# The first layer's gate in block form: half of its contraction as seven block products in place of eight

## Chip, core and metric

One core of one Trainium2 chip runs the whole program. The metric is the device time of one execution in microseconds (us). The engines are TensorE (PE in the profile), VectorE (DVE), ScalarE (ACT), GpSimd (POOL) and SyncE (SP); the last two issue most DMAs.

## What is computed

Two decoder layers over 512 tokens of width 1024 in float32. Layer 0 mixes tokens with a Mamba-2 SSD, layer 1 with HGRN2. Behind each mixer come a squared-ReLU MLP and a gated embedding:

```python
h = layer_norm(ALPHA * x + mix, ln_g[i, 0], ln_b[i, 0])
h = layer_norm(ALPHA * h + sq_relu_mlp(h, w1[i], w2[i]), ln_g[i, 1], ln_b[i, 1])
x = h + sigmoid(h @ ple_w_gate[i]) * (p[i] @ ple_w_proj[i])
```

The change is in the last line for i = 0: the gate's product h @ ple_w_gate is 512x1024 by 1024x1024, and the projection of p has a contraction of 256.

## The kernel before

**Products.** Every float32 matrix is split in two float32r parts, hi (a rounded copy, made by ScalarE) and lo (the difference, made by VectorE). A product is three matmuls, hi by hi, hi by lo and lo by hi (mm3, L120 to L122), 128 contraction rows by 128 tokens by 512 columns each. A weight unit is 128x1024: SyncE loads it into one of three buffers raw, then split makes whi (L113, ScalarE) and wlo (L116, VectorE) in rings of six. PSUM has four banks pj and one each of pt, pm, py0 and py1.

**Block products.** The MLP's second product, the value projection (values4) and the last layer's gate (last_gate) use seven products of matrix blocks in place of eight (Strassen's scheme as Winograd orders it). It needs sums of weight blocks and sums of token blocks. weight_sums loads weight blocks with GpSimd's DMAs (L329) into the eight buffers r and sums them on VectorE (L336, L339, L340, L344). last_gate makes its four sums t3, t1, t2, t4 in the DMAs themselves: GpSimd issues them with an adding or copying DMA each (L401 to L408), and a link that adds to a buffer waits for the DMA that filled it.

**The gate of layer 0 before.** The end of mlp_and_gate runs two halves of 512 columns by four chunks of 128 tokens; each has 24 matmuls of the gate and 6 of the projection. Behind the next chunk's matmuls the finished chunk of x is transposed (turn, L625), four transposes for half a row, and split into x_n, with a plain copy in rows for values4's block sums. **The gate of layer 1**, last_gate, takes half of the contraction in seven block products (part), the other half directly (rest), and holds partial results in cells. The pair sums of h come from kept, a copy that transpose_split makes (L245).

**Around it.** The last period of the MLP's second product gives the layer norm its chunks: product accumulates into acc with row sums (L373), layer_norm finishes chunk by chunk (L213 to L224), and turned yields the transposes of h (L238, split on ScalarE in L242 and on VectorE in L243) between the gate's first matmuls. values4, the first part of layer 1, runs right behind layer 0's gate and needs its own weight sums.

**Order.** The engines run their queues in order. A list scheduler sets each engine's order ahead of the run by priorities (high_priority with LEAD 100, SOON 40 and so on) and its own estimates of durations; the part of the order that the change touches is shown below. A tile's buffer is given out when its last user is done.

Of the kernel before, what the change touches and what calls it, by code (L numbers as in the profile page):

```python
# [15 lines left out]
P = 128  # L16
T = 512
# [27 lines left out]
def trunk(ctx: ExitStack, tc, a):  # L45
# [351 lines left out]
    def last_gate(wp, wg, h_s, p_s, kept, turned):  # L397
# [13 lines left out]
        cells = [mk(b8, [P, 4, T], "b8") for _ in range(3)] + [tmp("blk", [P, 4, T])]  # L411
        cell = lambda n: cells[n // 4][:, n % 4, :]
# [36 lines left out]
        def final(c, h, g, pp, pin=None):  # L449
# [3 lines left out]
            for ps, cs in pp:  # L453
# [5 lines left out]
                nc.sync.dma_start(a["out"][tok(c), fs], acc[:, c, fs])  # L459
# [46 lines left out]
        raw = mk(raws, [P, 1024], "raw")  # L506
        pu = mk(w4, [P, 1024], "a", F32R), mk(w4, [P, 1024], "b", F32R)
        with tc.high_priority(offset=LEAD):
            nc.sync.dma_start(raw, wp[1])
            nc.scalar.copy(pu[0], raw)  # L510
            nc.vector.tensor_sub(pu[1], raw, f32(pu[0]))
# [15 lines left out]
        for u in range(2):  # L527
# [3 lines left out]
            final(2 + u, 0, cell(6 + u), [(cell(2 + u), whole)])  # L531
        for u in range(2):
# [25 lines left out]
    def mlp_and_gate(layer, h_s, last):  # L558
# [36 lines left out]
        for g, period in enumerate(PERIODS):  # L595
            if g < 4:
                tiles = hidden(g)
            if g > 0:
                if g == 4:
                    kept = tmp("blk", [P, 2, 4, 256]) if last else None  # L600
# [12 lines left out]
        if last:  # L613
            return last_gate(a[f"wp_{layer}"], a[f"wg_{layer}"], h_s, p_s, kept, turned)

        x_n = Split(8)
        rows = [tmp("blk", [P, 2, 4, 256]) for _ in range(2)]
        late = []

        def turn(h, c):  # L620

            sl = slice(c * P, (c + 1) * P)
            pt = bank(pst, "pt")
            for j in range(4):
                nc.tensor.transpose(pt[:, j * P : (j + 1) * P], acc[:, c, h * 512 + j * P : h * 512 + (j + 1) * P], ident)  # L625
            v = pt.rearrange("p (j t) -> p j t", j=4)
            hh = x_n.hi[h][:, :, sl]
            nc.scalar.copy(hh, v)
            nc.scalar.copy(rows[c // 2][:, h, :, c % 2 * P : (c % 2 + 1) * P], v)
            nc.vector.tensor_sub(x_n.lo[h][:, :, sl], v, f32(hh))  # L630

        pps = {}

        def proj(c, pu):

            ps = pps[c] = bank(*((psj, "pj") if c > 1 and pps else (psy, "py%d" % (c % 2))))
            sl = slice(c * P, (c + 1) * P)
            for k in range(2):
                ks = slice(k * 512, (k + 1) * 512)
                mm3(ps, p_s[0][:, k, sl], p_s[1][:, k, sl], pu[0][:, ks], pu[1][:, ks], k == 0, k == 1)  # L640

        for h in range(2):
            pu = unit(a[f"wp_{layer}"][h])
            gu = [unit(a[f"wg_{layer}"][4 * h + j]) for j in range(4)]
            for c in range(NCH):
                sl = slice(c * P, (c + 1) * P)
                if h == c == 0:
                    turns = turned(1)
                    for i in range(NCH):
                        proj(i, pu)  # L650
                        if i in (1, 2):
                            next(turns)
                if h == 1:
                    proj(c, pu)
                turns = turned(c + 2) if h == 0 and c < 2 else None
                pg = bank(psj, "pj")
                sg = tmp("sg", [P, T])
                for k in range(8):
                    ks = slice((k % 2) * 512, (k % 2 + 1) * 512)
                    mm3(pg, h_s.h(k, sl), h_s.l(k, sl), gu[k // 2][0][:, ks], gu[k // 2][1][:, ks], k == 0, k == 7)  # L660
                    if turns and k in (2, 5):
                        next(turns)
                nc.scalar.activation(sg, pg, AF.Sigmoid)
                nc.vector.tensor_mul(sg, pps.pop(c), sg)
                d = acc[:, c, h * 512 : (h + 1) * 512]
                nc.vector.tensor_add(d, sg, d)
                while late:
                    late.pop(0)()
                late.append(lambda h=h, c=c: turn(h, c))
        return x_n, rows, late  # L670

    def values4(xs, rows, late):
# [38 lines left out]
        for f in late:  # L711
            f()
# [751 lines left out]
```

## Time and profile before

| what | value |
|---|---|
| time, median of 3 runs | 1411.65 us (1411.61 to 1413.34) |
| the profiled execution | 1411.34 us |
| its span, first to last instruction | 1409.6 us |
| TensorE busy | 1404.3 us, 8001 matmul records |
| VectorE busy | 1069.1 us |
| ScalarE busy | 763.6 us |
| GpSimd busy | 45.8 us |
| HBM over the span | 127 GB/s |

Times within a profile are counted from the span's start. A line number names the source line of an instruction, and "out<-in" the tiles it writes and reads. The time in square brackets behind a row is how long its engine stood idle before it, and what ended that. Layer 0's gate begins near 696 us and values4 near 760; the last gate is the end of the program, from 1347 us on.

### The profile page before, as it was taken

Reading aid. Unit: us, or ns where it says so; the run is one execution under the profiler, and the core shown is the slowest. Engines: PE = TensorE matmul, PEld = TensorE weight load, DVE = VectorE, ACT = ScalarE, POOL = GpSimd, SP = SyncE. Lnnn points to the kernel's source line nnn. Section 1 sums busy time; section 2 is a strip of 40 time slices with the busy share of each in tenths; the row PEclk is TensorE's granted clock in tenths of the full one; section 3 lists DMA queues with packets and bytes.
Section 4 is the critical chain, followed back from the end, with each engine's and each line's share of the span. In section 5 each row is a group of like instructions: output and inputs, shape, how many; then the busy total and the mean of one; then the engine's idle time right before and its main releaser. Section 6 shows DMA issues by size and latency. Waiting matters only on the chain.

```text
span 1409.6 us, 20400 instructions
## 1 busy us (share of the span) xinstructions
PE 1404.3 (100%) x8001; PEld 1168.1 (83%) x8001; DVE 1069.1 (76%) x1778; ACT 763.6 (54%) x1156; POOL 45.8 (3%) x92
## 2 busy tenths in 40 slices
PE   9999999999999999999999999999999999999998
PEld 7888888888988888888888888888898888888887
DVE  7989688698977668677986577678785867667795
ACT  7766465573354444545555547655555454544573
POOL 0000000001000000000000000000100000000100
PEclk9999999999999999999999999999999999999999
DMA  8433333234433444345621421222443444444731
GB/s 313 135 117 120 106 120 110 85 100 156 141 113 127 157 131 152 129 142 178 209 90 49 134 91 61 76 87 96 150 135 105 147 137 148 144 137 159 202 106 60
DMA packets 50399, 181.69 MB, mean 129 GB/s; under 512 B 5632, under 2 KB 6400, under 8 KB 50176
## 3 DMA queue, kind: packets, MB, share of 16 engines
q1 hardware_dynamic: 38784, 138.45, 29.6%
q0 software_dynamic: 11520, 41.95, 9.2%
q8 instruction: 63, 1.03, 0.3%
q14 instruction: 32, 0.26, 0.1%
HBM read 177.16 MB, written 2.16 MB: 127 GB/s over the span
## 4 chain that ended last, share of the span: by engine, by line
PE 99%; DMA 0%; DVE 0%; issue 0%; DVEq 0%
PE pj L120 25%; PE pj L121 25%; PE pj L122 25%; PE py L120 5%; PE py L122 5%; PE py L121 5%; PE py L906 1%; PE pt L238 1%; PE py L1175 1%; PE pm L923 1%; PE pm L871 1%; PE py L1301 1%; PE pt L859 0%; PE py L1303 0%; PE py L1240 0%; PE py L832 0%
## 5 line engine op out<-in xcount | busy, mean ns | idle before, releaser
L113 ACT CAST whi<-raw 128x1024 fp32r<-128x1024 f32 x218 | 228.8, 1050 | 333.2 <-PE pj L121 243.6
L120 PE MATMUL pj<-b,whi 128*128 128x512 f32 (+1 forms) x990 | 378.6, 383 | 0.0
L122 PE MATMUL pj<-b,wlo 128*128 128x512 f32 (+1 forms) x990 | 376.8, 381 | 0.0
L121 PE MATMUL pj<-b,whi 128*128 128x512 f32 (+1 forms) x990 | 376.6, 381 | 0.0
L116 DVE TENSOR_TENSOR wlo<-raw,whi 128x1024 fp32r<-128x1024 f32 x218 | 265.4, 1221 | 129.4 <-ACT whi L113 128.2
L121 PEld LDWEIGHTS pj<-b,whi 128*128 128x128 f32 x990 | 186.4, 188 | 34.6 <-issue 0.9
L122 PEld LDWEIGHTS pj<-b,wlo 128*128 128x128 f32 x990 | 186.3, 188 | 34.5
L120 PEld LDWEIGHTS pj<-b,whi 128*128 128x128 f32 x990 | 186.1, 188 | 34.0
L122 PE MATMUL pj<-whi,b 128*128 128x512 f32 x520 | 204.1, 392 | 0.0
L120 PE MATMUL pj<-whi,b 128*128 128x512 f32 x508 | 202.1, 398 | 0.0
L121 PE MATMUL pj<-wlo,b 128*128 128x512 f32 x508 | 199.2, 392 | 0.0
L113 ACT CAST whi<-r 128x1024 fp32r<-128x1024 f32 x76 | 80.0, 1053 | 68.5 <-PE pj L122 39.4
L122 PEld LDWEIGHTS pj<-whi,b 128*128 128x128 f32 x520 | 97.7, 188 | 20.1
L120 PEld LDWEIGHTS pj<-whi,b 128*128 128x128 f32 x508 | 95.5, 188 | 19.1 <-ACT b L1322 0.3
L121 PEld LDWEIGHTS pj<-wlo,b 128*128 128x128 f32 x508 | 95.5, 188 | 18.7 <-issue 0.2
L116 DVE TENSOR_TENSOR wlo<-r,whi 128x1024 fp32r<-128x1024 f32 x76 | 92.5, 1220 | 19.6 <-ACT whi L113 19.1
L122 PE MATMUL py<-whi,b 128*128 128x512 f32 x260 | 101.3, 390 | 0.0
L121 PE MATMUL py<-wlo,b 128*128 128x512 f32 x248 | 96.6, 389 | 0.0
L120 PE MATMUL py<-whi,b 128*128 128x512 f32 x248 | 96.4, 390 | 0.0
L329 POOL DMA_DIRECT2D r<-in_w x64 | 34.0, 532 | 1098.8 <-DVE wlo L116 544.3
L122 PEld LDWEIGHTS py<-whi,b 128*128 128x128 f32 x260 | 48.8, 188 | 10.2
L800 DVE SCALAR_TENSOR_TENSOR cv<-pj,cst,cv 128x509 f32<-128x509 f32 (+2 forms) x66 | 48.9, 746 | 10.6 <-ACT cv L797 9.8
(368 smaller groups left out, 1943.5 us busy)
## 6 DMA issues: line engine op xcount, KB each, us to landing
raw<-in_w SPq DMA_DIRECT2D x112, 512.0 KB, 3.3
r<-in_w POOLq DMA_DIRECT2D x64, 512.0 KB, 3.8
raw<-in_wssd SPq DMA_DIRECT2D x36, 512.0 KB, 3.9
a<-csd SPq DMA_DIRECT2D x16, 512.0 KB, 4.1
raw<-in_wso SPq DMA_DIRECT2D x16, 512.0 KB, 3.3
raw<-in_whq SPq DMA_DIRECT2D x16, 512.0 KB, 3.4
raw<-in_wg SPq DMA_DIRECT2D x15, 512.0 KB, 4.0
raw<-in_whvg SPq DMA_DIRECT2D x14, 512.0 KB, 3.4
```

The costliest lines, as they stand in the source:

```text
L113: nc.scalar.copy(hi[:, :n], f)
L116: nc.vector.tensor_sub(lo[:, :n], f, f32(hi[:, :n]))
L120: nc.tensor.matmul(out, sh, mh, start=start, stop=False, **kw)
L121: nc.tensor.matmul(out, sh, ml, start=False, stop=False, **kw)
L122: return nc.tensor.matmul(out, sl, mh, start=False, stop=stop, **kw)
L238: nc.tensor.transpose(pt[:, j * P : (j + 1) * P], src[:, k * P : (k + 1) * P], ident)
L329: queue.dma_start(t[i][u], src)
L800: nc.vector.scalar_tensor_tensor(cv[:, d:], ps[:, : T - d], convw[:, i, k : k + 1], cv[:, d:], ALU.mult, ALU.add)
L871: nc.tensor.matmul(pst_[:, c * P : (c + 1) * P], btok[:, c, :], xw[:, c].rearrange("p h q -> p (h q)"), start=True, stop=True)
L906: mm = nc.tensor.matmul(yds[0][64 * r : 64 * r + 64, sl], xdt[:, 2 * c + r, :], m[:, r, sl], start=True, stop=True)
L923: mm = nc.tensor.matmul(yo[:, c * P : (c + 1) * P], pv[:, c - 1].rearrange("p h q -> p (h q)"), cm[:, c * P : (c + 1) * P], start=True, st ...
L1175: nc.tensor.matmul(pcs[r][bs, at : at + n], kk[r][:, ts], qs, start=True, stop=True)
```

## The change

last_gate becomes block_gate with an argument last and serves both layers. For layer 0 it keeps the new x in acc in place of writing it out, holds its partial results in two tiles of cells in place of four, computes the projection's second half just before each use, and transposes the new x (turn) between its own products. The two last turns are left to values4, which places them inside its first products. kept exists in both layers now. The layer norm of layer 0 ahead of the gate has priority SOON for all chunks.

```diff
-            with tc.high_priority(offset=LEAD if c == 3 and i % 2 == 0 else 0 if c > 1 and i == 1 else SOON):
+            with tc.high_priority(offset=LEAD if c == 3 and i % 2 == 0 else SOON):
...
-    def last_gate(wp, wg, h_s, p_s, kept, turned):
+    def block_gate(wp, wg, h_s, p_s, kept, turned, last):
...
+        if last:
+            cells = [mk(b8, [P, 4, T], "b8") for _ in range(3)] + [tmp("blk", [P, 4, T])]
+            cell = lambda n: cells[n // 4][:, n % 4, :]
+        else:
+            cells = [mk(b8, [P, 4, T], "b8"), tmp("blk", [P, 4, T])]
+            homes = [(0, 0), (0, 1), (0, 2), (0, 3), (1, 0), (1, 1), (0, 0), (0, 1), (1, 2), (1, 3)]
+            cell = lambda n: cells[homes[n][0]][:, homes[n][1], :]
...
-        raw = mk(raws, [P, 1024], "raw")
-        pu = mk(w4, [P, 1024], "a", F32R), mk(w4, [P, 1024], "b", F32R)
...
-        for n, c in enumerate((2, 3, 0)):
-            ps = bank(psj, "pj")
-            proj(ps, c, pu)
-            nc.scalar.copy(cell(10 + n), ps)
+        if last:
...
         for u in range(2):
+            if not last and u:
+                turn(0, 2)
             part(x[u], summed(2), t1, u, False)
             nc.vector.tensor_add(cell(8 + u), x[u], cell(8 + u))
         us = [negated(wg[6]), negated(wg[7])]
         b22 = unit(wg[5])
+        if not last:
+            pu = unit(wp[1])
+            for u in range(2):
+                g = bank(psj, "pj")
+                rest(g, 2 + u, us, True)
+                nc.vector.tensor_add(cell(8 + u), g, cell(8 + u))
+                ps = bank(psj, "pj")
+                proj(ps, 2 + u, pu)
+                final(2 + u, 1, cell(8 + u), [(ps, whole)])
+                if u == 0:
+                    turn(0, 3)
+            for u in range(2):
+                part(x[u], summed(3), b22, u, False, False)
+                if u:
+                    turn(0, 1)
+                rest(x[u], u, us, False)
+                if u == 0:
+                    turn(0, 0)
+                ps = bank(psj, "pj")
+                proj(ps, u, pu)
+                final(u, 1, x[u], [(ps, whole)])
+                turn(1, 2 + u)
+            return x_n, rows, [lambda: turn(1, 0), lambda: turn(1, 1)]
...
-        x_n = Split(8)
-        rows = [tmp("blk", [P, 2, 4, 256]) for _ in range(2)]
...
-        for h in range(2):
-            pu = unit(a[f"wp_{layer}"][h])
-            gu = [unit(a[f"wg_{layer}"][4 * h + j]) for j in range(4)]
-            for c in range(NCH):
...
+        return block_gate(a[f"wp_{layer}"], a[f"wg_{layer}"], h_s, p_s, kept, turned, last)
...
             for c in range(2):
+                if late and c:
+                    late.pop(0)()
...
-        for f in late:
-            f()
+        late.pop(0)()
```

The source lines shift by the change: L336 to L344, L373 and the L401 to L408 of the sums keep their numbers; the negation of a weight unit (negated) is L425 and L427 before and L430 and L432 after, and the pair sums of h are L497 to L503 before and L503 to L509 after. In the rows below the numbers behind a name tell buffers apart, and a trailing "xn" counts equal rows.

First, GpSimd's queue between the last sums of the MLP and the memory fills of layer 1. r is a buffer of a weight block, in_wg the gate's weight, in_whvg that of the value projection. Before:

```order
L329 DMA r_5542<-in_w_0 128x1024
L329 DMA r_6347<-in_whvg 128x1024
L329 DMA r_6341<-in_whvg 128x1024
L329 DMA r_6343<-in_whvg 128x1024
L329 DMA r_6348<-in_whvg 128x1024
L329 DMA r_6342<-in_whvg 128x1024
L329 DMA r_6344<-in_whvg 128x1024
L329 DMA r_6345<-in_whvg 128x1024
L329 DMA r_6346<-in_whvg 128x1024
```

Now, up to the fourth load of the value projection:

```order
L401 DMA r_5889<-in_wg 128x1024
L403 DMA r_5889<-in_wg 128x1024
L402 DMA r_5890<-in_wg 128x1024
L405 DMA r_5891<-r_5889 128x1024
L404 DMA r_5890<-in_wg 128x1024
L406 DMA r_5891<-in_wg 128x1024
L407 DMA r_5892<-r_5891 128x1024
L329 DMA r_6388<-in_whvg 128x1024
L329 DMA r_6382<-in_whvg 128x1024
L408 DMA r_5892<-in_wg 128x1024
L329 DMA r_6384<-in_whvg 128x1024
L329 DMA r_6389<-in_whvg 128x1024
```

The eight loads of the value projection stood alone there; now the gate's chain stands ahead of them, with two of the loads before its last link and the third behind it.

Second, VectorE's queue at the end of the MLP's second product, at the first sums for the value projection. wlo is the low part of a weight unit, lnsum the row sums of the layer norm, lnmv its mean and variance, pj and py are banks. Before:

```order
L336 TENSOR_TENSOR r_6341<-r_6341,r_6347 128x1024
L336 TENSOR_TENSOR r_6342<-r_6342,r_6348 128x1024
L116 TENSOR_TENSOR wlo_5811<-raw_5807,whi_5809 128x1024
L116 TENSOR_TENSOR wlo_5817<-raw_5813,whi_5815 128x1024
L373 ISA acc_99,lnsum_5530<-pj_5610,acc_99 128x512
L373 ISA lnsum_5530 128x1
L373 ISA acc_99,lnsum_5530<-py_940_5573,acc_99 128x512
L373 ISA lnsum_5530 128x1
L339 TENSOR_TENSOR r_6347<-r_6347,r_6343 128x1024
L116 TENSOR_TENSOR wlo_5897<-raw_5893,whi_5895 128x1024
L213 TENSOR_SCALAR lnmv_5739<-lnsum_5530 128x1
L116 TENSOR_TENSOR wlo_5903<-raw_5899,whi_5901 128x1024
```

Now:

```order
L336 TENSOR_TENSOR r_6382<-r_6382,r_6388 128x1024
L339 TENSOR_TENSOR r_6388<-r_6388,r_6384 128x1024
L116 TENSOR_TENSOR wlo_5812<-raw_5808,whi_5810 128x1024
L116 TENSOR_TENSOR wlo_5818<-raw_5814,whi_5816 128x1024
L373 ISA acc_99,lnsum_5531<-pj_5611,acc_99 128x512
L373 ISA lnsum_5531 128x1
L373 ISA acc_99,lnsum_5531<-py_941_5574,acc_99 128x512
L373 ISA lnsum_5531 128x1
L340 TENSOR_TENSOR r_6384<-r_6382,r_6384 128x1024
L116 TENSOR_TENSOR wlo_5909<-raw_5905,whi_5907 128x1024
L116 TENSOR_TENSOR wlo_5915<-raw_5911,whi_5913 128x1024
L373 ISA acc_99,lnsum_5531<-py_942_5575,acc_99 128x512
```

The second sum there now is L339, which reads the third load (r_6384), where an L336 on the fourth and fifth loads' buffers stood; L340 follows, and the norm's first row (L213) has moved behind the accumulations.

Third, TensorE's queue in layer 0's gate, behind the last transposes of h. whi and wlo are the parts of a weight unit, b the parts of h or of its pair sums, pt a bank of transposes. Before, the end of the second chunk's product with the turn of the first chunk of x:

```order
L122 MATMUL pj_6059<-whi_5919,b_921_5529 128x512
L120 MATMUL pj_6059<-whi_5919,b_919_5527 128x512
L121 MATMUL pj_6059<-wlo_5921,b_919_5527 128x512
L122 MATMUL pj_6059<-whi_5919,b_921_5529 128x512
L625 MATMUL pt_6088<-cst_165,acc_99 128x128 x4
L120 MATMUL pj_6096<-whi_5901,b_918_5526 128x512
L121 MATMUL pj_6096<-wlo_5903,b_918_5526 128x512
L122 MATMUL pj_6096<-whi_5901,b_920_5528 128x512
```

Now, the end of the block product with t2, the first two matmuls of rest with the negated unit, and the block product with t4:

```order
L122 MATMUL py_1031_5983<-whi_6092,b_1005_5901 128x512
L120 MATMUL py_1031_5983<-whi_6092,b_1005_5901 128x512
L121 MATMUL py_1031_5983<-wlo_6094,b_1005_5901 128x512
L122 MATMUL py_1031_5983<-whi_6092,b_1005_5901 128x512
L120 MATMUL pj_6229<-whi_6207,b_920_5528 128x512
L121 MATMUL pj_6229<-wlo_6209,b_920_5528 128x512
L120 MATMUL pj_6104<-whi_6096,b_919_5527 128x512
L121 MATMUL pj_6104<-wlo_6098,b_919_5527 128x512
L122 MATMUL pj_6104<-whi_6096,b_921_5529 128x512
```

Two matmuls of the third chunk's rest, which need the low part wlo_6209 of a negated unit, stand ahead of the block product with t4.

The low part that the second of them reads stands here in VectorE's queue now, behind the sums of pairs (blk) and their low parts (b_1005, b_1006), with no counterpart before:

```order
L504 TENSOR_TENSOR blk_5522<-blk_5522 128x512
L116 TENSOR_TENSOR wlo_6102<-r_5890,whi_6100 128x1024
L499 TENSOR_TENSOR b_1005_5901<-blk_5522,b_1005_5901 128x512
L506 SCALAR_TENSOR_TENSOR blk_5522<-blk_5522 128x512
L499 TENSOR_TENSOR b_1006_5902<-blk_5522,b_1006_5902 128x512
L509 SCALAR_TENSOR_TENSOR blk_5522<-blk_5522 128x512
L499 TENSOR_TENSOR b_1005_5901<-blk_5522,b_1005_5901 128x512
L492 TENSOR_TENSOR blk_5904<-pj_6038,blk_5904 128x512
L336 TENSOR_TENSOR r_6383<-r_6383,r_6389 128x1024
L499 TENSOR_TENSOR b_1006_5902<-blk_5522,b_1006_5902 128x512
L461 TENSOR_TENSOR sg_6084<-b_1007_5903,sg_6084 128x512
L432 SCALAR_TENSOR_TENSOR wlo_6209<-raw_6205,whi_6207 128x1024
```

L432 is the twelfth row from L504, with a sum for the value projection (L336) and the first gate result (L461) ahead of it.

More of the change, by code (lines that the diff above doesn't have):

```diff
@@ L504, in last_gate @@
             put(3, a12)
[L506 to L515 removed]
+        if last:
+            raw = mk(raws, [P, 1024], "raw")
+            pu = mk(w4, [P, 1024], "a", F32R), mk(w4, [P, 1024], "b", F32R)
+            with tc.high_priority(offset=LEAD):
+                nc.sync.dma_start(raw, wp[1])
+                nc.scalar.copy(pu[0], raw)
+                nc.vector.tensor_sub(pu[1], raw, f32(pu[0]))
+            for n, c in enumerate((2, 3, 0)):
+                ps = bank(psj, "pj")
+                proj(ps, c, pu)
+                nc.scalar.copy(cell(10 + n), ps)
         for u in range(2):
@@ L531, in last_gate, with turn @@
             final(2 + u, 0, cell(6 + u), [(cell(2 + u), whole)])
+        x_n = Split(0)
+        rows = [None, None]
+        def turn(h, c):
+            if len(x_n.hi) == h:
+                x_n.hi.append(mk(b8, [P, 4, T], "b8", F32R))
+                x_n.lo.append(mk(b8, [P, 4, T], "b8", F32R))
+            if rows[c // 2] is None:
+                rows[c // 2] = tmp("blk", [P, 2, 4, 256])
+            pt = bank(pst, "pt") if c % 2 else bank(psm, "pm")
+            for j in range(4):
+                nc.tensor.transpose(pt[:, j * P : (j + 1) * P], acc[:, c, h * 512 + j * P : h * 512 + (j + 1) * P], ident)
+            v = pt.rearrange("p (j t) -> p j t", j=4)
+            hh = x_n.hi[h][:, :, tok(c)]
+            nc.scalar.copy(hh, v)
+            nc.scalar.copy(rows[c // 2][:, h, :, c % 2 * P : (c % 2 + 1) * P], v)
+            nc.vector.tensor_sub(x_n.lo[h][:, :, tok(c)], v, f32(hh))
         for u in range(2):
+            if not last and u:
+                turn(0, 2)
             part(x[u], summed(2), t1, u, False)
@@ L599, in mlp_and_gate @@
                 if g == 4:
-                    kept = tmp("blk", [P, 2, 4, 256]) if last else None
+                    kept = tmp("blk", [P, 2, 4, 256])
                     h_s, after, turned, sums = norm(2 * layer + 1, kept)
```

50 lines of the change are left out of this document (2 added, 48 removed).

## The prediction

> **What bounds the kernel now.** I read the page first: the span, the busy times, the chain that ended last.
>
> ```profile
> span 1409.6 us, 20400 instructions
> ...
> PE 1404.3 (100%) x8001; PEld 1168.1 (83%) x8001; DVE 1069.1 (76%) x1778; ACT 763.6 (54%) x1156; POOL 45.8 (3%) x92
> ...
> PE 99%; DMA 0%; DVE 0%; issue 0%; DVEq 0%
> ```
>
> TensorE (PE) is the whole chain: 99% of it, with no share for a wait. A busy PE need not be a fast one, so next comes PE's timeline at two places, the products of the last gate and the turns before the first one.
>
> ```profile
> 1370.14 0.39 PE L120 MATMUL pj<-a,a 128*128 128x512 f32 x1
> ...
> 1374.22 0.39 PE L120 MATMUL pj<-whi,b 128*128 128x512 f32 x1
> ...
> 695.64 0.39 PE L122 MATMUL py<-whi,blk 128*128 128x512 f32 x1
> 695.87 0.60 PE L238 MATMUL pt<-cst,acc 128*128 128x128 f32 x4
> 696.23 0.48 PE L120 MATMUL py<-whi,blk 128*128 128x512 f32 x1
> 696.54 0.40 PE L121 MATMUL py<-wlo,blk 128*128 128x512 f32 x1
> ```
>
> The first column is the start. Eighteen matmuls lie between 1370.14 and 1374.22: 0.227 us each, start to start. A turn of four transposes with the matmul behind it takes 695.87 to 696.54, so the turn alone costs 0.44 us. These are steps without a wait. What the change saves on PE it saves in full, and whatever makes PE wait is added in full.
>
> Which engine could make it wait is told by the busy time by stretch, around the start of the first gate and the same place in the last one.
>
> ```profile
> 680.00:690.00 10.00, 10.00 (x46) 8.28 (x45) 9.80 (x14) 5.20 (x7) 0.00 (x0) 1.00 0.63 210
> 690.00:700.00 10.00, 10.00 (x48) 8.27 (x47) 10.00 (x19) 6.83 (x13) 0.00 (x0) 1.00 0.63 205
> ...
> 1330.00:1340.00 10.00, 10.00 (x46) 8.28 (x45) 6.53 (x14) 4.57 (x8) 0.86 (x1) 1.00 0.95 312
> ```
>
> After the length come PE, weight loads, VectorE (DVE), ScalarE, GpSimd, PE's clock, DMA share and GB/s. DVE is full ahead of the first gate and has 3.5 us in 10 free ahead of the last, because the sums of the value projection's weights (L336 to L344) run only in the first layer. The last gate's form comes to a place where DVE has nothing to spare.
>
> **Part by part: PE.** The removed gate has 8 chunks (2 halves by 4) of 30 matmuls, 240. The block form has 7 block products of 12, the direct half of the contraction (96) and the projection of p (48): 228. Twelve fewer at 0.227 us are 2.72 us. The turns stay 8 in number. DVE and ScalarE get four more weight splits, the cell copies and the pair sums; these cost nothing where the engine has room, and DVE has none up to the first pair.
>
> **The load that DVE waits for.** The GpSimd queue issues these loads one after another.
>
> ```profile
> 653.38 0.53 POOL L329 DMA_DIRECT2D r<-in_whvg  x1 [19.87 <-DVE wlo L116]
> ...
> 675.03 0.53 POOL L329 DMA_DIRECT2D r<-in_whvg  x1 [1.20 <-DVE wlo L116]
> ...
> 1304.75 0.53 POOL L401 DMA_DIRECT2D r<-in_wg  x1 [20.86 <-DVE wlo L116]
> 1308.75 0.90 POOL L403 DMA_DIRECT2D r<-in_wg  x1 [3.47 <-DMA r<-in_wg]
> ...
> 1320.74 0.87 POOL L406 DMA_DIRECT2D r<-in_wg  x1 [3.87 <-DMA r<-r]
> 1327.10 0.57 POOL L407 DMA_DIRECT2D r<-r  x1 [5.49 <-issue]
> 1333.24 0.86 POOL L408 DMA_DIRECT2D r<-in_wg  x1 [5.57 <-DMA r<-r]
> ```
>
> Today the eight value loads (L329) start from 653.38, as buffers come free; the last is issued at 675.03. The last gate's sums are a chain, each link waiting for the landing before it, from L401 at 1304.75 to L408 at 1333.24. Both start when the same buffers of the last product come free, so the layers lie 1304.75 - 653.38 = 651.37 apart. In the first layer the chain therefore issues L407 at 675.7 and L408 at 681.9, done at 682.7. By the order, two value loads stand ahead of L408 and the third, r_6384, right behind it: it can't be issued before 682.7.
>
> What it takes to land is bounded by these rows: the page's median of such loads, then the answers for L402 and L404 (a plain load issued just behind an accumulating one, and an accumulating one behind a copy).
>
> ```profile
> r<-in_w POOLq DMA_DIRECT2D x64, 512.0 KB, 3.8
> ...
> DMA to landing us min/median/max: 6.2/6.2/6.2
> ...
> DMA to landing us min/median/max: 8.0/8.0/8.0
> ```
>
> r_6384 is a plain load behind the accumulating L408, so I take L402's 6.2 us: it lands at 688.9. The ends are 686.5 and 690.7.
>
> DVE's timeline of before at that place:
>
> ```profile
> 680.46 2.36 DVE L336 TENSOR_TENSOR r<-r,r 128x1024 f32<-128x1024 f32 x2
> 682.73 2.36 DVE L116 TENSOR_TENSOR wlo<-raw,whi 128x1024 fp32r<-128x1024 f32 x2
> ...
> 688.78 0.20 DVE L213 TENSOR_SCALAR lnmv<-lnsum 128x1 f32<-128x1 f32 x1
> ...
> 690.75 0.15 DVE L218 TENSOR_TENSOR lnmv<-lnsq 128x1 f32<-128x1 f32 x1
> 690.82 1.27 DVE L223 SCALAR_TENSOR_TENSOR acc<-acc,lnmv,a 128x1024 f32<-128x1024 f32 x1
> ...
> 692.80 1.28 DVE L224 SCALAR_TENSOR_TENSOR acc<-acc,lnrs,b 128x1024 f32<-128x1024 f32 x1
> ...
> 1368.96 0.68 DVE L243 TENSOR_TENSOR b<-pm,b 128x512 fp32r<-128x512 f32 x1
> 1369.56 0.68 DVE L493 TENSOR_TENSOR b<-blk,b 128x512 fp32r<-128x512 f32 x1
> ```
>
> Steps, start to start: 1.14 us for 1024 columns (680.46 to 682.73 for two), 0.60 for 512 (1368.96 to 1369.56), 1.2 for a layer norm's 1024-wide step. In the new order the second row after 680.46 is an L339 that reads r_6384. Undisturbed it ends at 682.7; with the load at 688.9 it ends at 690.1, 7.4 us later. Behind it wait the splits of the last MLP product's units, the accumulations of its banks and the first chunk's layer norm. From 680.46 undisturbed: seven steps of 1.14 and three of 0.6 to L213, 690.3; 2.0 to the variance (688.78 to 690.75), then three norm steps of 1.2, one of 0.6 and small ones: the norm ends at 696.7. PE reaches the first turn, now six matmuls later than 695.87, at 697.2. So 0.5 us of the 7.4 is covered and **6.9 us** reach PE; with the ends of the landing, 4.5 and 8.7.
>
> **DVE at the first pair.** PE's rows from the first turn to the first block product on a pair are 78 matmuls and 8 turns, 17.7 + 3.5 = 21.2 us. DVE's rows from that norm's end to the last sum before that pair (L504) are 5 of 1.2, 6 of 1.14, 13 of 0.6 and 0.6 us of small ones: 21.3, and the cast on ScalarE behind it takes another 0.6. PE waits 0.9. The last gate doesn't show this wait because its 18 projection matmuls (1370.14 to 1374.22, 4.1 us) stand just there; in the new code they come later. Then PE runs 24 matmuls (5.4 us) and a first one of the negated rest; the second needs L432's output, behind two steps of 1.14 and eight of 0.6 since L504 and itself 1.14: with one 0.7 us wait for a cast, 8.9 us after L504, where PE arrives after 0.8 + 5.7 = 6.5. PE waits 2.4 more. Together **3.3 us**. Ends: 1.0, if one wait of ScalarE shifts and the second disappears, and 4.5, if the following three weight sums also get in the way of the first turn of x.
>
> **The sum.** -2.7 + 6.9 + 3.3 = +7.5 us. The profiled execution took 1411.34 us (1.74 outside the span); its median of three is 1411.65, 0.3 more. Forecast: **1418.8 us**. Its own range: 1411.34 - 2.7 + 4.5 + 1.0 = 1414.1 to 1411.34 - 2.7 + 8.7 + 4.5 = 1421.8.
>
> **The clock.** The 6.9 us fall into pieces. The longest comes after the bank of the first turn's MLP product is free: PE runs six matmuls (1.4 us) while DVE does the norm's 6.4 from L213 to the end, so it stands for 5.0. How PE begins after standing still is seen at the kernel's start.
>
> ```profile
> 0.78 3.36 PE L153 MATMUL pm<-const-float32-0.0 128*128 128x256 f32 x8 [0.78 <-PEq L1452]
> ...
> L153 PE MATMUL pm<-const-float32-0.0 x8: 381/634/767, 0.8 to 3.8; 128*128 128x256 f32 x8
> ```
>
> Eight equal matmuls; most last 634 ns, the last one 381. If PE began so again after the wait, 3.36 us of work at 634 in place of 381 would lose 3.36 x (1 - 381/634) = 1.3 us. The Trainium skill ("TensorE: Matmul & The Clock Gate", Part 1) says that an idle window of about 3.4 us halves PE's clock until it has been busy about as long; by that rule the loss here would be 1.7 us as an estimate from the page. No idle stretch of that length lies inside this trace, so it is a rival and not in the sum.
>
> **Rivals.**
> 1. Faster or even: the waits don't happen, and only the twelve matmuls count, 1408.6. It decides if r_6384 lands by 681.6, when L339 would begin undisturbed. For: the eight value loads are all issued by 675.03 now, and no L336 or L339 of that place waits. Against: six links of the chain would have to be over 7 us shorter in sum than the rows of the last gate, with the same buffers and the same neighbours. 0.12, of which I put 0.07 on just over 0.2% and 0.05 on just under.
> 2. The load comes in time but DVE is late at the first pair: -2.7 + 3.3 = +0.6, 1411.9. For: DVE's full stretch. Against: as under 1. 0.08.
> 3. The forecast and the clock: 1418.8 + 1.3 = 1420.1. For: L153's rows. Against: the wait is split by the rest of an MLP product, and its one long piece is hardly longer than the warm-up of the start. 0.12.
> 4. That PE's matmuls don't get fewer is ruled out by the order, which has twelve fewer of 128x512.
>
> **How the numbers follow.** The forecast has 0.68. Runs of this kernel tell 0.2%, 2.8 us, from no change. Slower: the forecast and rival 3, 0.80. Within 0.2%: rival 2 and part of rival 1, 0.13. Faster: 0.07. The range leaves out rival 1 (0.12) and the tails: from 1411.8, just below rival 2, to 1423.0, the forecast's upper end with the clock's 1.3.
>
> **What would show it.** Right: in the profile after, an L339 of DVE shortly after 680 idle for 5 to 9 us, ended by a DMA of in_whvg; PE idle ahead of the first L238 of the first layer for about as long; L408 of the first layer starting near 682 and the L329 behind it landing near 689; PE waiting 1 us at the first block product with t3 and 2 to 3 us at the first rest with negated weights; 12 matmuls fewer. Wrong: the L339 without idle time before it (the load term falls), the wait there but PE running on (DVE had slack that I didn't see), or PE's steps in this gate longer than 0.227 us without a wait.

## Result and profile after

| what | before | after |
|---|---|---|
| time, median of 5 runs each | 1412.28 us (1411.61 to 1413.34) | 1424.75 us (1424.66 to 1426.14) |
| ratio after to before | | 1.0091, 95% interval 1.0076 to 1.0106 |
| the profiled execution | 1411.34 us | 1426.14 us |

The kernel became 12.5 us slower, 0.9%. The prediction said slower, but by 7 us: 1418.8, with a range up to 1423.0. Three lines of the page after answer to those of before: the span, the busy times, and the chain that ended last.

```profile
span 1423.9 us, 20423 instructions
...
PE 1409.8 (99%) x7989; PEld 1170.0 (82%) x7989; DVE 1081.6 (76%) x1797; ACT 774.4 (54%) x1177; POOL 51.5 (4%) x100
...
PE 48%; DVE 2%; DMA 1%; issue 1%; ACT 0%; POOL 0%; DVEq 0%; POOLq 0%
```

Twelve matmul records fewer (7989, 8001 before), and yet more busy time on PE: some matmuls became longer. The chain, all PE before, now passes through DVE and a DMA. (It could be followed back from the end only to 670.65 us, so its shares add up to about half.) Where it does so, PE's timeline shows (start, duration; in brackets the idle time before and what ended it):

```profile
693.95 0.39 PE L122 MATMUL pj<-whi,b 128*128 128x512 f32 x1
697.57 0.77 PE L120 MATMUL py<-whi,blk 128*128 128x512 f32 x1 [3.23 <-DVE lnsum L373]
698.14 0.63 PE L121 MATMUL py<-wlo,blk 128*128 128x512 f32 x1
...
703.23 0.39 PE L121 MATMUL py<-wlo,blk 128*128 128x512 f32 x1
...
704.15 0.40 PE L122 MATMUL py<-whi,blk 128*128 128x512 f32 x1
707.76 1.11 PE L238 MATMUL pt<-cst,acc 128*128 128x128 f32 x4 [3.21 <-DVE acc L224]
708.53 0.78 PE L120 MATMUL py<-whi,blk 128*128 128x512 f32 x1
...
713.63 0.40 PE L120 MATMUL pj<-whi,a 128*128 128x512 f32 x1
```

Two waits of 3.2 us, and behind each a stretch of slow matmuls: 13 from 697.57 to 703.23 and 12 from 708.53 to 713.63, 0.43 us a step in place of 0.227. The clock column of the stretches agrees (length, PE, weight loads, DVE, ScalarE, GpSimd, clock, DMA share, GB/s):

```profile
680.00:690.00 10.00, 10.00 (x46) 8.29 (x45) 2.81 (x5) 2.11 (x2) 1.96 (x3) 1.00 1.01 339
690.00:700.00 10.00, 6.77 (x26) 5.25 (x25) 7.29 (x10) 2.10 (x2) 0.00 (x0) 0.82 0.57 192
700.00:715.00 15.00, 11.79 (x39) 9.18 (x38) 13.61 (x27) 9.67 (x20) 0.00 (x0) 0.67 0.37 113
```

The first of these rows holds the origin. DVE, full there before, works 2.8 us in 10, and the DMA engines, at 0.63 before, are at 1.01. DVE's timeline says what it waits for, GpSimd's when those loads were issued:

```profile
681.50 0.08 DVE L373 DVE_READ_ACCUMULATOR2_ANT lnsum<- 128x1 f32 x1
687.35 1.23 DVE L336 TENSOR_TENSOR r<-r,r 128x1024 f32<-128x1024 f32 x1 [5.77 <-DMA r<-in_whvg]
692.71 1.23 DVE L339 TENSOR_TENSOR r<-r,r 128x1024 f32<-128x1024 f32 x1 [4.14 <-DMA r<-in_whvg]
...
676.66 0.55 POOL L407 DMA_DIRECT2D r<-r  x1 [5.14 <-DVE wlo L116]
677.29 1.08 POOL L329 DMA_DIRECT2D r<-in_whvg  x2
682.57 0.89 POOL L408 DMA_DIRECT2D r<-in_wg  x1 [4.20 <-DMA r<-r]
683.12 1.41 POOL L329 DMA_DIRECT2D r<-in_whvg  x2
```

Not one sum waits but two. The times from issue to landing of the two pairs of L329:

```profile
DMA to landing us min/median/max: 6.2/7.8/9.5
...
DMA to landing us min/median/max: 9.5/9.9/10.2
```

Three smaller waits follow: at the first block product with t3, at the second matmul of the rest with a negated unit, and at a turn of the new x.

```profile
732.67 0.50 PE L120 MATMUL pj<-whi,b 128*128 128x512 f32 x1 [0.64 <-ACT b L498]
...
740.19 0.50 PE L121 MATMUL pj<-wlo,b 128*128 128x512 f32 x1 [1.31 <-DVE wlo L432]
...
777.16 0.63 PE L551 MATMUL pt<-cst,acc 128*128 128x128 f32 x4 [0.83 <-DVE b L556]
```

**The account.** Steps from start to start, less the 0.227 us of a matmul without a wait: 3.4 and 3.4 for the two waits, 2.7 for the first slow stretch (5.66 for 13 matmuls, less 2.95), 2.7 for the second (0.3 at the transposes, then 5.10 for 12 matmuls, less 2.72), and 0.8, 1.6 and 1.0 at the three small ones: 15.6 us. Less 2.7 for the twelve matmuls that is 12.9, against 12.5 between the medians. The account is that of the profiled execution, whose span is 14.3 us longer than before. Of these, 1.0 lies at the program's start, far from the change: the first L120 begins at 8.57 us there and at 7.59 before. Between two marks, the first py<-whi,blk well ahead of the gate and the first py<-qd,cv behind it, it takes 349.9 us for 336.6 before, 13.3 more; the account explains all but 0.4 of that.

### The profile page after: what moved, and what is told of

Same layout as the page of the kernel before. It is cut to its first block, busy times and chain, and to the rows that moved or that the text cites. A ratio compares the mean times of both kernels' runs of the same rounds, so it can differ in the third digit from the quotient of the medians.

```text
span 1423.9 us, 20423 instructions
## 1 busy us (share of the span) xinstructions
PE 1409.8 (99%) x7989; PEld 1170.0 (82%) x7989; DVE 1081.6 (76%) x1797; ACT 774.4 (54%) x1177; POOL 51.5 (4%) x100
## 4 chain that ended last, share of the span: by engine, by line
PE 48%; DVE 2%; DMA 1%; issue 1%; ACT 0%; POOL 0%; DVEq 0%; POOLq 0%
PE pj L120 12%; PE pj L121 12%; PE pj L122 12%; PE py L122 3%; PE py L121 3%; PE py L120 3%; PE py L1170 1%; DMA r<-in_whvg 1%; PE pt L238 1%; DVE wlo L116 1%; PE py L1296 1%; DMA r<-r 0%; PE py L1298 0%; PE py L1235 0%; PE py L1278 0%
## 5 line engine op out<-in xcount | busy, mean ns | idle before, releaser
L120 PE MATMUL pj<-b,whi 128*128 128x512 f32 (+1 forms) x990 | 378.6, 383 | 0.0
L116 DVE TENSOR_TENSOR wlo<-raw,whi 128x1024 fp32r<-128x1024 f32 x215 | 261.6, 1221 | 130.2 <-ACT whi L113 129.3
L120 PEld LDWEIGHTS pj<-b,whi 128*128 128x128 f32 x990 | 186.2, 188 | 34.3
L122 PE MATMUL pj<-whi,b 128*128 128x512 f32 x504 | 198.0, 393 | 0.0
L120 PE MATMUL pj<-whi,b 128*128 128x512 f32 x480 | 191.4, 399 | 0.6 <-ACT b L498 0.6
L121 PE MATMUL pj<-wlo,b 128*128 128x512 f32 x480 | 188.3, 392 | 1.3 <-DVE wlo L432 1.3
L113 ACT CAST whi<-r 128x1024 fp32r<-128x1024 f32 x80 | 84.2, 1054 | 69.2 <-PE pj L122 39.1
L122 PEld LDWEIGHTS pj<-whi,b 128*128 128x128 f32 x504 | 95.0, 188 | 20.1 <-DVE b L556 0.4
L116 DVE TENSOR_TENSOR wlo<-r,whi 128x1024 fp32r<-128x1024 f32 x80 | 97.4, 1219 | 17.5 <-ACT whi L113 17.1
L121 PE MATMUL py<-wlo,b 128*128 128x512 f32 x272 | 106.1, 390 | 0.0
L120 PEld LDWEIGHTS pj<-whi,b 128*128 128x128 f32 x480 | 90.2, 188 | 19.3 <-ACT b L498 1.1
L121 PEld LDWEIGHTS pj<-wlo,b 128*128 128x128 f32 x480 | 90.2, 188 | 19.2 <-DVE wlo L432 1.6
L122 PE MATMUL py<-whi,b 128*128 128x512 f32 x272 | 106.0, 390 | 0.0
L120 PE MATMUL py<-whi,b 128*128 128x512 f32 x272 | 105.8, 390 | 0.0
L329 POOL DMA_DIRECT2D r<-in_w x64 | 34.0, 532 | 1104.4 <-DVE wlo L116 544.5
L120 PEld LDWEIGHTS py<-whi,b 128*128 128x128 f32 x272 | 51.1, 188 | 10.7
L122 PEld LDWEIGHTS py<-whi,b 128*128 128x128 f32 x272 | 51.1, 188 | 10.6
```

What stands on the lines that cost most here:

```text
L113: nc.scalar.copy(hi[:, :n], f)
L116: nc.vector.tensor_sub(lo[:, :n], f, f32(hi[:, :n]))
L120: nc.tensor.matmul(out, sh, mh, start=start, stop=False, **kw)
L121: nc.tensor.matmul(out, sh, ml, start=False, stop=False, **kw)
L122: return nc.tensor.matmul(out, sl, mh, start=False, stop=stop, **kw)
L329: queue.dma_start(t[i][u], src)
```

## Experiments

The theory after the comparison has two parts. A: value loads stand in GpSimd's queue behind a chain of DMAs, DVE waits in order for sums that PE needs only some 80 us later, and PE waits for DVE. B: the chain and these loads fill the DMA engines just where the gate's own loads come. The rivals are named in the expectations. Each kernel below is the changed kernel with one edit; ratios are to the kernel before, whose median was 1412.2 to 1412.3 in all groups. In some kernels line numbers are shifted by up to 20. The diffs show the lines that make the difference; lines that only carry a value from one place to another are left out.

**1. Four value loads ahead of the chain's last link (loads_ahead).**

```diff
+            if not last:
+                early.append({i: [tmp("r", [P, 1024]) for _ in range(2)] for i in (2, 1, 3, 0)})
+                v = a["whvg"]
+                for i, u, n in ((0, 0, 4), (2, 0, 6), (1, 0, 0), (0, 1, 5)):
+                    nc.gpsimd.dma_start(early[0][i][u], v[n])
             nc.gpsimd.dma_start(t4, wg[1], accum_op=ALU.add)
```

> Only GpSimd's queue is changed: the four first value loads stand ahead of the last link of the gate's sums (L408) in place of two ahead and two behind; DVE's order is the same, word for word. Theory A, the place in the queue (the load behind the last link can't be issued until that link is): the third value load goes out near 678.5 in place of 683.1 and lands near 688, right when L336 is released, so the second wait of DVE (4.1 us at L339) shrinks to 1 us or less, the PE waits by as much, and the time falls by 3 to 5 us to 1420 to 1422. Rival B, the transfers share the DMA engines (their share is 1.02 in that stretch), so that loads issued earlier land no earlier: L339 is released at 691 or later and the time stays within 1.5 us of 1424.8. Under both, DVE's first wait (5.8 us at L336) stays at 5 to 7 us.

Measured: 1422.31 us, ratio 1.0069 (1.0056 to 1.0082). GpSimd's queue, the landings of the four loads, and DVE:

```profile
677.09 2.16 POOL L415 DMA_DIRECT2D r<-in_whvg  x4
...
DMA to landing us min/median/max: 8.3/11.1/13.0
...
687.96 1.23 DVE L339 TENSOR_TENSOR r<-r,r 128x1024 f32<-128x1024 f32 x1 [6.75 <-DMA r<-in_whvg]
690.27 1.23 DVE L342 TENSOR_TENSOR r<-r,r 128x1024 f32<-128x1024 f32 x1 [1.08 <-DMA r<-in_whvg]
```

The third load went out 4.9 us earlier (678.2 for 683.1) and DVE got it 2.4 us earlier (690.27 for 692.71). The second wait almost vanished, but the first grew by 1.0, and the four loads took up to 13.0 us. The gain of 2.4 us lies between A's and B's, and its interval overlaps that of the change. Both parts act: a place ahead in the queue is half lost again on full DMA engines.

**2. All eight sums behind the gate's pair sums (sums_later).**

```diff
-        t1, t2, t3, t4 = weight_sums(w, VALUE_SUMS)
+        t1, t2, t3, t4 = weight_sums(w, VALUE_SUMS, after=late_sums[0])
```

(late_sums[0] is the last lo part that put makes in the gate.)

> All eight sums of the value weights are put behind the last pair sum of h on DVE; the loads, the chain and PE's program stay. Theory A, DVE waits in order for loads that PE doesn't need yet: both DVE waits vanish (9.9 us), with them PE's two waits of 3.2 us and the two stretches at half clock, and with 3.4 us less of DVE's work ahead of the first pair the waits at the first block product with t3 and at the second negated rest shrink below 0.8 us in sum: about 1411 (1409.6 to 1413). Rival C, DVE's volume ahead of the first pair sets the time whatever the loads do: PE still waits 2 to 3.5 us there, 1413 to 1415. Rival D, the sums are now late for the value products: a PE wait ahead of the product with the first value sum, over 1 us.

Measured: 1416.67 us, ratio 1.0034 (1.0021 to 1.0048): 8.1 us of the 12.5 are gone, not all, and the time lies above A's range. The waits for value loads and the first long PE wait vanished, and there is no wait at the first pair, so C falls; there is none at the value products either (D). But PE still waits at the first turn (and 1.4 us at a turn of x near 768), and DVE for splits of the weights that SyncE loads. The longest of these waits is for the MLP's last unit, not for the gate's own weights. The last row has the landings of SyncE's three loads L106 issued from 679 to 686, one each for the MLP, the projection and the gate:

```profile
700.03 1.11 PE L239 MATMUL pt<-cst,acc 128*128 128x128 f32 x4 [3.03 <-DVE acc L224]
...
688.22 1.22 DVE L116 TENSOR_TENSOR wlo<-raw,whi 128x1024 fp32r<-128x1024 f32 x1 [3.22 <-ACT whi L113]
...
DMA to landing us min/median/max: 8.0/8.6/9.8
```

SyncE's three loads of that window before, and without the crowd (experiment 7 below, loads_later); there they are one for the projection and two for the gate:

```profile
DMA to landing us min/median/max: 3.2/4.4/5.2
...
DMA to landing us min/median/max: 4.7/5.2/5.6
```

**3 and 4. Five sums later, and fourteen matmuls in the wait (five_later, five_later_fill).**

```diff
-                with behind(after):
+                with behind(after if u >= free else None):
...
+                        for _ in range(14):
+                            with tc.issue_after(ins.ins), tc.high_priority(offset=SOON):
+                                ins = nc.tensor.matmul(warmed[0], t[:, 0, k, sl], w_[0], start=True, stop=True)
```

> The first three value sums stay where they are, the five others are put behind the last pair sum of h on DVE. Theory A: the loads' waits are the same as after the change (two DVE waits of 5.8 and 4.1 us, two PE waits of about 3.2 us, two stretches at half clock); only one L336 of 1.14 us goes from ahead of the second negated unit, so its wait falls from 1.6 to about 0.5 us: 1423.0 to 1424.0. It is also the partner of the next kernel. Rival C (DVE's volume behind the first turns matters more than the loads): 1421 or less.

> The kernel before this one with 14 more matmuls of 128x512 (14 x 0.227 = 3.2 us, written to a free bank that nobody reads) just ahead of the first transposes of h, where PE stands for 3.2 us. Theory A, the clock falls to half by that wait and costs time of its own: with the fillers the matmuls behind the wait step 0.227 us in place of 0.427, 11 x 0.2 = 2.2 us less, so 14 matmuls more make the kernel 1.5 to 2.5 us faster than its partner. Rival E, the clock costs nothing there because DVE is late by as much at the first pair: the same time within 0.7 us. Rival F, the fillers are in the way: slower by up to 3 us.

Measured: 1424.45 (ratio 1.0086, 1.0072 to 1.0100) and 1425.11 us (1.0089, 1.0075 to 1.0103). five_later is the changed kernel again, within its interval: the five other sums are not the matter, and C falls here too. Its trace isn't the one that was expected, though, and its time lies 0.5 us above the range of A: PE waits 2.17, 1.01 and 4.61 us up to the first turn, only the last with a slow stretch behind it, and 1.1 us for the second negated unit. The fillers didn't pay, but the trace doesn't decide between A and E:

```profile
706.89 0.66 PE L240 MATMUL pt<-cst,acc 128*128 128x128 f32 x4 [1.08 <-DVE acc L224]
...
714.42 1.12 PE L240 MATMUL pt<-cst,acc 128*128 128x128 f32 x4 [2.95 <-ACT blk L247]
715.19 0.78 PE L122 MATMUL pj<-whi,b 128*128 128x512 f32 x1
```

At the spot the fillers did as meant: 1.08 us of wait and no slow matmul behind it. But the scheduler had also moved other work, and the next turn now waited 2.95 us for ScalarE, with a slow stretch of its own. What the clock costs by itself is not shown by this pair; experiment 5 shows it. The four runs of five_later_fill hint at it: two with a mean granted clock of 1.000 took 1423.06 and 1424.32 us, and two with 0.998 and 0.997, the profiled one among them, 1426.12 and 1425.89 us.

**5. The chain replaced by four plain loads (plain_chain).**

```diff
+            else:
+                nc.gpsimd.dma_start(t3, wg[4])
+                nc.gpsimd.dma_start(t1, wg[5])
+                nc.gpsimd.dma_start(t2, wg[0])
+                nc.gpsimd.dma_start(t4, wg[1])
```

> The first gate's eight DMAs that make t3, t1, t2, t4 are replaced by four plain loads of weight blocks, one for each tile; the sums are left out, so the output is not the reference's. DVE's order up to the first turn is the same, the first two value sums ahead of the last MLP splits included. Theory A+B (the chain of adding DMAs holds GpSimd's queue until 683 and fills the DMA engines until 691): the four free buffers get their value loads between 670 and 678, these land by 683, and raw loads of the gate take 3 to 5 us again; DVE's waits of 5.8 and 4.1 us fall below 2 us in sum; about 1413 to 1416, where the order of the two first norms still costs PE a wait at the first turn. Rival H (the order of DVE's instructions alone is too slow, whatever the DMAs do): 1421 or more, with PE's two waits of 3 us in place.

Measured: 1413.73 us, ratio 1.0010 (1.0001 to 1.0019). DVE's order is the same up to the first norms, and its two sums don't wait:

```profile
681.14 1.22 DVE L336 TENSOR_TENSOR r<-r,r 128x1024 f32<-128x1024 f32 x1
682.40 1.23 DVE L339 TENSOR_TENSOR r<-r,r 128x1024 f32<-128x1024 f32 x1
```

H falls: 11 of the 12.5 us come from the chain of DMAs. (The kernel leaves out the four sums, so it tells only where the time goes.) The first turn came without a wait as well; left are 0.6, 1.3 and 0.8 us at the three small places.

This kernel also shows what the second slow stretch of the changed kernel costs, and so answers rival E of experiments 3 and 4. In both kernels the first turn starts within 0.3 us of the end of its norm. From there to the first block product with t3, PE and DVE have the same rows in the same order, but here PE has no slow stretch. The first two rows are PE's in plain_chain, the third is DVE's in the changed kernel:

```profile
697.91 0.60 PE L238 MATMUL pt<-cst,acc 128*128 128x128 f32 x4
...
720.20 0.50 PE L120 MATMUL pj<-whi,b 128*128 128x512 f32 x1 [0.60 <-ACT b L504]
...
715.81 0.69 DVE L243 TENSOR_TENSOR b<-pt,b 128x512 fp32r<-128x512 f32 x1 [1.24 <-ACT b L242]
```

PE takes 22.3 us here and 24.9 in the changed kernel (707.76 to 732.67), 2.6 more, though the wait at the end of it is as long in both (0.60 and 0.64). The stretch isn't hidden by a late DVE: PE's turns come later, ScalarE and DVE wait for them, and DVE is idle for 2.5 us on this way in place of 0.4. E's condition, that DVE is late by as much anyway, doesn't hold.

**6. The first line of the change undone (late_priority).**

```diff
-            with tc.high_priority(offset=LEAD if c == 3 and i % 2 == 0 else SOON):
+            with tc.high_priority(offset=LEAD if c == 3 and i % 2 == 0 else 0 if c > 1 and i == 1 else SOON):
```

> Only the first line of the change is undone: the layer norm of chunks 2 and 3 ahead of the first gate has no priority again. The loads, the chain and the two early value sums stay. Theory A+B: the waits at L336 and L339 are ahead of all norms and stay as they are, so 1423.5 to 1426. Rival G (the new priority of chunks 2 and 3 is what makes chunk 0's norm late): under 1421.

Measured: 1424.66 us, ratio 1.0078 (1.0064 to 1.0091). Both waits are still there, the first 1.2 us shorter, and G falls:

```profile
685.10 1.23 DVE L336 TENSOR_TENSOR r<-r,r 128x1024 f32<-128x1024 f32 x1 [4.59 <-DMA r<-in_whvg]
690.64 1.23 DVE L339 TENSOR_TENSOR r<-r,r 128x1024 f32<-128x1024 f32 x1 [4.32 <-DMA r<-in_whvg]
```

**7. Value loads later, too (loads_later).** On top of sums_later:

```diff
+        if not last:
+            early.append({i: [tmp("r", [P, 1024]) for _ in range(2)] for i in (2, 1, 3, 0)})
+            with tc.high_priority(offset=SOON):
+                for i, u in ((0, 0), (2, 0), (1, 0), (0, 1)):
+                    nc.vector.tensor_copy(early[0][i][u][:, 0:1], acc[:, 3, 0:1])
```

> As sums_later, and the value loads too are later: four copies of one column on DVE, behind the last norm, write to the first four value buffers, so that GpSimd can load them only then (near 715). sums_later left a PE wait of 3.0 us at the first turn; in its trace the gate's raw loads on SyncE took 8 to 10 us between 679 and 690 (3.2 to 5.2 before), and ScalarE and DVE waited for them in order. Theory B, the value loads crowd the gate's own loads on the DMA engines: raw loads at 3 to 5.5 us again, the wait at the first turn under 1.5 us and no stretch at half clock; with -2.7 for the matmuls and about 1.2 for the one wait at a turn of x near 770: 1410.5 to 1412.5. Rival I, the norms of chunks 0 and 1 run through each other on DVE and the first is late by itself: the wait at the first turn stays at 2.5 us or more with a stretch at half clock, 1414 to 1417.

Measured: 1413.10 us, ratio 1.0005 (0.9997 to 1.0014), 3.6 us less than sums_later. DVE's order up to the last norm is that of sums_later, SyncE's loads take 4.7 to 5.6 us (shown under 2), and PE has no wait from 675 to 760. So B holds. I falls: the norms of chunks 0 and 1 still run through each other (L224 twice from 694.35 on), and the turn isn't late. The time missed its 1410.5 to 1412.5 by 0.6, because the one wait left was larger than the 1.2 us expected and had a slow stretch behind it:

```profile
694.35 2.47 DVE L224 SCALAR_TENSOR_TENSOR acc<-acc,lnrs,b 128x1024 f32<-128x1024 f32 x2
...
762.46 1.01 PE L559 MATMUL pt<-cst,acc 128*128 128x128 f32 x4 [2.00 <-DVE b L564]
763.12 0.78 PE L122 MATMUL py<-whi,b 128*128 128x512 f32 x1
```

**8. Two priorities more (all_mended).**

```diff
-            with tc.high_priority(offset=LEAD if c == 3 and i % 2 == 0 else SOON):
+            with tc.high_priority(offset=LEAD if c == 3 and i % 2 == 0 or c == 0 and i == 1 else SOON):
...
+            with tc.high_priority(offset=LEAD):
+                nc.vector.tensor_sub(x_n.lo[h][:, :, tok(c)], v, f32(hh))
```

> As loads_later, and two priorities: chunk 0's norm ahead of the first gate stands before other work on DVE (so that chunks 0 and 1 no longer run through each other), and the lo parts of the turned x are made at once, so that the bank pt comes free. If the list of causes is whole, all waits of the first gate go and the twelve matmuls are left: 1409 to 1411, faster than before by 0.1 to 0.2%. If one more cause is open, PE's waits in that gate are over 1.5 us in sum and the time is 1411.5 or more.

Measured: 1415.63 us, ratio 1.0020 (1.0011 to 1.0028), slower than without them. The list wasn't whole: the lo parts came early, and the gate's last addition, for which the last turn waits, came late. Which of the two priorities did that wasn't tested apart.

```profile
767.90 0.63 PE L559 MATMUL pt<-cst,acc 128*128 128x128 f32 x4 [3.61 <-DVE acc L471]
```

**9 and 10. DVE's order around the turns (two_sums_last, six_sums_last).** On top of loads_later, the gate's last products and additions and the lo parts of the turns get LEAD, and sums stand behind the last turn's lo part:

```diff
+        for f in later[:2]:
+            f()
+        for f in later[2:]:
+            with behind(turn_subs[0]):
+                f()
```

(For six_sums_last all six of later.)

> As loads_later (one PE wait left, 2.0 us at a turn of x at 760 and half clock behind it, ended by DVE's lo part of an earlier turn). DVE works without a pause from 735 to 766 there, so order within it decides: the lo parts of the turned x and the gate's last products and additions get a high priority, and the last two of the eight value sums are put behind the last turn's lo part. Theory K (DVE's order, not its volume, makes the turn late): no PE wait over 0.5 us in the gate, 12 matmuls fewer are left: 1409.5 to 1411. Rival L (volume: the wait only moves to the value product with the second sum, near 778): 1411.5 to 1414.

> As two_sums_last, with six of the eight value sums behind the last turn's lo part. Theory K: 1409.5 to 1411 too. Rival L: the turns of x go without a wait, but DVE has 6 x 1.14 = 6.8 us more to do between the last turn and the value product with the second sum, and PE waits there for 2 us or more: 1411.5 to 1414.

Measured: 1411.34 (ratio 0.9995, 0.9986 to 1.0004) and 1414.44 us (1.0018, 1.0010 to 1.0027). The page of the first, PE's one wait left in it, and the two waits of the second:

```profile
PE 1402.6 (100%) x7989; PEld 1165.2 (83%) x7989; DVE 1081.0 (77%) x1801; ACT 774.8 (55%) x1177; POOL 51.7 (4%) x100
...
776.07 0.50 PE L122 MATMUL py<-whi,b 128*128 128x512 f32 x1 [0.68 <-DVE b L702]
```

```profile
777.47 0.50 PE L120 MATMUL py<-whi,b 128*128 128x512 f32 x1 [0.79 <-ACT whi L113]
779.80 0.80 PE L121 MATMUL py<-wlo,b 128*128 128x512 f32 x1 [1.83 <-DVE wlo L116]
```

For two sums the answer lies between the theories. The gate itself is free of waits, as K has it, but 0.7 us of wait moved to the value product (L702 belongs to values4, and two value sums stand just ahead of it on DVE), as L has it, and the time lies between K's 1411 and L's 1411.5. L holds for six, where the backlog is handed on to the value product, with a time 0.4 us above its range. two_sums_last is the best version of the block form: none of the account's waits is left, and there is a new one of 0.7. Its median is 0.8 us below before, which its interval doesn't tell from no change. Of the 2.7 us of the matmuls, 2.0 should be left. Between the marks of the account its trace is 1.3 us shorter than before (335.2 for 336.6); where the rest is stays open, within the spread of the runs (1410.30 to 1412.70).

## Why the prediction was wrong

Slower was right; the size was not. Two steps failed: the landing of the third value load, taken as 6.2 us and measured as 9.5, and the clock, which the sum left out and which cost 2.7 us. The terms in order:

**PE, -2.7.** Right in the count, 12 matmul records fewer. The time isn't shown in full: two_sums_last, almost without waits, has PE busy for 1402.6 us, 1.7 less than before, and 2.0 less between the marks of the account.

**The load that DVE waits for, +6.9.** The mechanism was right and its size was off: PE lost 9.5 us up to the first turn (3.4, 2.7 and 3.4 of the account; the first slow stretch is in it: DVE's rows up to the norm's end at 707.7 show no wait for PE, so the norm would have ended no earlier for a fast one). The chain came as laid out: L408 at 682.57 (forecast 681.9), the load behind it at 683.12. The term that failed is the landing, "I take L402's 6.2 us": 9.5, beyond the upper bound of 8.0. For most of its time that row's load had one other transfer beside it, the link L403 issued 0.6 us ahead. Here three value loads (this one among them), the last link and two of SyncE's loads were in flight together within 0.6 us of its issue, at a share of 1.01. The share alone doesn't tell the two apart: it was 0.92 there too (1310 to 1315 us, before). The step "two value loads stand ahead of L408" counted their place and not their bytes: they landed late themselves, and the first of DVE's two waits (5.8 us at L336) is theirs and wasn't foreseen. It cost nothing of its own here, since L339's load landed later still (683.12 and 9.5 us make 692.6). L339 ended at 693.86, 10.1 us later than 681.50 and two sums of 1.14 make it, in place of the 7.4 of the prediction. The 9.5 us that PE lost, less the 6.9, are 2.6 of the 5.4 us that the sum missed.

By the Trainium skill ("DMA: Bandwidth & Descriptors", Issuing engines are not separate DMA queues), DMAs from any engine run on the same 16 DMA engines and interleave. The rows of experiments 2 and 7 agree: SyncE's loads took 8.0 to 9.8 us beside GpSimd's value loads and 4.7 to 5.6 without them. The prediction spoke of GpSimd's queue alone and left SyncE's loads out; sums_later against loads_later shows their price, 3.6 us, once the first wait is out of the way.

**The clock, a rival with 1.3 us and 0.12.** It happened, and twice. The first slow stretch cost nothing by itself; the second cost 2.7 us in the account and 2.6 against plain_chain, a term that the sum put at nothing because the trace of before had no such idle stretch. The argument against it, that the wait is split and its longest piece hardly longer than the warm-up, was wrong: two pieces of 3.2 us did it. The Trainium skill ("TensorE: Matmul & The Clock Gate", Part 1) says that an idle window of about 3.4 us halves the clock, and that the window runs freely. The half speed agrees (0.427 for 0.227), but waits of 3.23 and 3.21 us were enough, in loads_later one of 2.00 us, and in six_sums_last one of 1.83 us just behind one of 0.79.

**DVE at the first pair, +3.3.** Right in place, smaller in size: 0.8 (forecast 0.9) at the first block product with t3, and 1.6 (forecast 2.4) at L432. The sum had put a wait of 0.7 us for a cast between L504 and L432, and DVE's rows from 731.23 to 740.1 show no idle time. The slow stretch isn't the reason: plain_chain, without one, has the same idle times there (0.60 and 1.3 us, for 0.64 and 1.31).

**Left out.** The turn of x at 777 waited 1.0 us for a lo part of DVE; the prediction's upper end named the first turn of x as late, the sum none. Together: 2.6 + 2.7 - 0.9 + 1.0 = 5.4, which leads from +7.5 to the account's 12.9.

**The rivals.** 1 and 2 (the load in time) are what plain_chain makes of the kernel; it is 1.4 us slower than before, where rival 2 had 0.6. Range: its top was the forecast's upper end and the clock's 1.3 (1423.1 in sum, not 1423.0), and fell with the bound of 8.0 us.

## What to carry to other kernels

When a change moves DMAs, add up the bytes in flight at the new place, of all queues, before taking a landing time from a row: a landing measured beside fewer transfers was too short here, 6.2 us for 9.5. Work that nobody needs soon (here sums for the next part of the program) should be held back, its loads too, until the engine that works in order has done what is needed now; with the chain in place both holds were needed here, 8.1 us for the sums and 3.6 for the loads. A form with fewer matmuls pays only as far as the engine that feeds it has room: even with every wait but 0.7 us taken away, 2.7 us less of matmuls gave a gain too small to measure here.

## What was not expected of the hardware

A 512 KB load, 3.8 us in the median of the page, took 8.3 to 13.0 us with four such loads, a link and SyncE's loads at once (loads_ahead). The length of a wait did not tell the length of the slow stretch behind it: 3.2 us were followed by 13 and 12 slow matmuls, 2.00 us (loads_later) by about 6, 4.61 us (five_later) by 4, 4.59 us at the same place in late_priority by 11, and 2.17 us in five_later by none. Nor is it the same in each run of a kernel: of the eleven runs of six_sums_last, the two with a mean granted clock of 1.000 took 1413.19 and 1413.65 us, and the five with 0.998 took 1414.44 to 1417.51 us. And the stretch need not begin at once: behind all_mended's wait of 3.61 us three matmuls ran at nearly full speed, then eight at half. The first three rows are all_mended's, the last three five_later's.

```profile
768.85 0.42 PE L122 MATMUL pj<-whi,b 128*128 128x512 f32 x1
769.08 0.61 PE L120 MATMUL pj<-whi,b 128*128 128x512 f32 x1
...
772.75 0.40 PE L120 MATMUL pj<-whi,b 128*128 128x512 f32 x1
...
706.12 1.12 PE L239 MATMUL pt<-cst,acc 128*128 128x128 f32 x4 [4.61 <-DVE acc L224]
...
695.87 0.47 PE L120 MATMUL py<-whi,blk 128*128 128x512 f32 x1 [2.17 <-DVE lnsum L374]
696.18 0.39 PE L121 MATMUL py<-wlo,blk 128*128 128x512 f32 x1
```
